# Joined at the seam of two layers and in the second: stores on another queue, value rows in three places, held loads

## The chip, the cores and the metric

The kernel runs on one core of one Trainium2 chip. The metric is device microseconds of one execution. Lower is better. Times of single executions are read from runs of the whole kernel, and where time goes is read from one profiled execution.

## What is computed

One step of a two-layer streaming encoder over 512 new prompt frames and 8 running streams of 16 frames each (640 rows of 2048). Layer 0 is stick-breaking attention with 16 heads and a cache; layer 1 is gated linear attention (GLA) with 4 heads, head widths 256 (keys) and 512 (values). The change touches the seam between the layers and layer 1:

```python
x = x + gate * y                                  # end of layer 0; per row
h = rmsnorm(x, norm_g) * (1 + scale) + shift      # start of layer 1
q, k, v, r, a_lr = split(h @ w_in)                # GLA products
g = log_sigmoid(a_lr @ w_a2 + b_a) / 16           # per-token decay
# Joined at the seam of two layers and in the second: stores on another queue, value rows in three places, held loads
a = tril((q * exp(b)) @ (k * exp(-b)).T)
o = a @ v + (q * exp(b)) @ S
S = exp(b_last) * S + (k * exp(b_last - b)).T @ v
```

Every float32 product is made of three matmuls on a high part and a low remainder (wh, wl, h and so on).

## The kernel before

One long function issues everything. TensorE's order (PE in the profile) is written out by a planner in the kernel: "lanes" are Python generators that yield a step with a wished delay, and a side scheduler puts their matmuls between those of the big products when the delay is over in its own count of time. The number in `step(2.8 ...)` is such a delay. ScalarE (ACT), VectorE (DVE) and GpSimd (POOL) keep the order that comes out of the recording in the parts around the change, and SyncE (SP) issues most DMAs in its order. Each engine works strictly in its own order, so an instruction that must wait holds up all that stands behind it on that engine. SP and ACT issue DMAs through hardware queues, POOL through a software queue (the helper `move`, L78). The DMAs of SP and ACT share a set of completion semaphores in rotation. A new DMA that gets a semaphore waits until the DMA that had it before has landed.

Three places matter.

**The seam (the part from L1235 on).** `add` (L1333) works on the 640 rows in five tiles (a = 0 to 4) and the 2048 columns in four groups (c = 0 to 3). VectorE makes x1 (L1336 to L1338), ScalarE sums its squares (L1340, tile junk) and then stores the tile to memory from its own queue (L1341, tile x<-y, 256 KB each, 20 in all). `turn` (L1316) lets TensorE transpose the tile (L1320) and ScalarE copy it out (L1322, xp). After the last group `norm` (L1325) reduces the squares (L1328), takes the root on VectorE and GpSimd (L232, L234, L243) and has TensorE turn the row factors (L248). ScalarE also casts the weights of layer 0's output product (L134, wh<-wr), and VectorE makes their remainder (L135, wl). `most` (L1295) prepares layer 1's input for rows 128 and up, `rest` that of the first 128 rows.

**The value jobs.** Layer 1's input product goes job by job, one of 256 output columns each (L595 matmuls, 170 a job). ScalarE's copy `m` (L608) stands once in each job. After a value job `keep_value` (L1451) has TensorE transpose the result in three pieces (g = 0, 1, 2; L681, ten transposes), ScalarE casts each into a tile kr and VectorE makes the remainder (L135, kr<-ps_tp,kr). SP stores both from kr (L74, gv<-kr, six stores a job). All three pieces use the same two slots, 12 and 13, so a piece can only be cast when the stores of the piece before have landed. Between these steps VectorE prepares the weights of the job after: t (L558), wb (L559, L562), and combines products: u and out (L601). The pool w5 (L1492) holds the tiles wa2r and wa2, which are used ahead of the value jobs only.

**The start of the GLA stage.** Here the last products (L654, copies pl at L1528, stores gq<-pl from ScalarE's queue at L1530) run beside the lanes `decays` (L1627 on: sums and exponentials of the gates of one head, es at L1673, for two halves dt = 0, 1), `prompt_lane` and `sample_lane` (L1819 on). SP loads v, q, k, three gate tiles (L1602) and weights (wr). POOL loads the first eight recurrent states (L1808, s<-in_state_gla, 256 KB each) and value rows of the samples (vst).

Of the kernel before, what the change touches and what calls it, by code (L numbers as in the profile page):

```python
# [26 lines left out]
GH = 4  # L27
# [14 lines left out]
def hybrid_step_kernel(ctx: ExitStack, tc: tile.TileContext, A: dict, O: list):  # L42
# [1200 lines left out]
    with tc.tile_pool(name="o0", bufs=1, reuse_waits="tile") as po, ExitStack() as only_d:  # L1243
# [81 lines left out]
        def norm(a):  # L1325
            yield step(3.0)
            ss = po.tile([P, 1], F32, tag="ss", name="ss", bufs=2)
            dve.tensor_reduce(out=ss, in_=ss4[:, a, :], axis=mybir.AxisListType.X, op=ALU.add)  # L1328
            wide = wide_of(po, rstd_of(po, ss, D, "nrm"))
            yield step(2.8 if a else 4.5, tp=1)  # L1330
            turned_wide(wide, bc, a)

        def add(a, c, pt):  # L1333
            xs, g = got[c]
            y = y_t[a, c]
            dve.tensor_tensor(y, pt, y, op=ALU.add)  # L1336
            dve.tensor_tensor(y, y, g[:, a // 4, :], op=ALU.mult)
            dve.tensor_tensor(y, y, xs[a], op=ALU.add)  # L1338
            junk = pd.tile([P, 512], BF16, tag="junk", name="junk", bufs=1)
            act(junk, y, AF.Square, accum_out=ss4[:, a, c:c + 1])  # L1340
            nc.scalar.dma_start(out=x1_d[a][:, 512 * c:512 * c + 512], in_=y)  # L1341
            if c == 3:
                side.add(counted(norm(a), a))
            side.add(counted(turn(a, c, y), a))
            busy["of"] += c > 0
# [105 lines left out]
        def keep_value(h, n):  # L1451
            def leave(out):
                def f(g, m, tp):
                    parts = [slot(12 + d, (P, 2, 256), name="kr")[:, :m, :] for d in range(2)]
                    halves(*parts, tp)
                    for d in range(2):
                        dst = gv_d[h][d][256 * g:256 * g + P * m, 256 * n:256 * n + 256]
                        store(dst.rearrange("(a p) n -> p a n", p=P), parts[d].bitcast(F32))
                side.add(as_rows(out, f))
            return leave  # L1460
# [28 lines left out]
        ring3["n"] = 1  # L1489
        ring3["pool"] = only_d.enter_context(tc.tile_pool(name="w2", bufs=1, reuse_waits="tile"))  # L1490

        wa_in = only_d.enter_context(tc.tile_pool(name="w5", bufs=1, reuse_waits="tile"))  # L1492
        r, wa2 = (wa_in.tile([96, GH * 256], t, name=n) for n, t in (("wa2r", F32), ("wa2", F32R)))
        for n in range(6):
            load(r[16 * n:16 * n + 16, :], A["gla_w_a2"][0])
        nc.scalar.copy(wa2, r)
# [20 lines left out]
    with tc.tile_pool(name="gl", bufs=1, reuse_waits="tile") as gl, \  # L1517
# [79 lines left out]
            act(on, o, AF.Copy, scale=r)  # L1597
            return on

        def gate(h, t0, tag, bufs):  # L1600
            g = gl.tile([P, 4, P], F32, tag=tag, name="gate", bufs=bufs)
            load(g, gr_d[h][:, :, t0:t0 + P])  # L1602
            return g

# [22 lines left out]
        def decays():  # L1627
# [8 lines left out]
            for h in range(GH):  # L1636
# [11 lines left out]
                for dt in range(2):  # L1648
                    n = 2 * h + dt
                    ba = cols[:, 48 + n:49 + n]  # L1650
                    b, y = (gl.tile([P, T], F32, tag=n, name=n) for n in ("b", "y"))
                    for c in hs:
                        yield step(0.0, tp=1)
                        pt = bank("tp")[:, :HALF]
                        l = wa2[:, P * dt:P * dt + P]
                        mm(pt, l, by(l, alr[:, c]), start=True, stop=True)
                        act(b[:, c], pt, AF.Abs, bias=ba)
                        dve.tensor_scalar(y[:, c], pt, ba, 0.0, op0=ALU.add, op1=ALU.min)
                    yield step(0.8)
                    act(b, b, AF.Exp, scale=-1.0)  # L1660
                    act(b, b, AF.Ln, bias=1.0)
                    yield step(1.7)
                    dve.tensor_tensor(y, y, b, op=ALU.subtract)
                    dve.tensor_tensor_scan(b, reset, y, 0.0, ALU.mult, ALU.add)
                    yield step(1.7)
                    bp = b[:, :NP].rearrange("p (c t) -> p c t", t=P)
                    bs = b[:, NP:].rearrange("p (c t) -> p c t", t=NT)
                    b1 = bp[:, :, 63:64].rearrange("p c o -> p (c o)")
                    bl = bp[:, :, 127:128].rearrange("p c o -> p (c o)")
                    act(e1[:, dt], b1, AF.Exp, scale=IT)  # L1670
                    act(el[:, dt], bl, AF.Exp, scale=IT)
                    dve.tensor_tensor(ed[:, dt], bl, b1, op=ALU.subtract)
                    act(es[:, dt], bs[:, :, 15:16].rearrange("p c o -> p (c o)"), AF.Exp, scale=IT)  # L1673
                    m = gl.tile([P, 4], F32, tag="m", name="m")
                    dve.tensor_copy(m, b1)
                    act(ed[:, dt], ed[:, dt], AF.Exp, scale=IT)
                    dve.tensor_tensor(bp, bp, m.unsqueeze(2).to_broadcast([P, 4, P]), op=ALU.subtract)
                    yield step(0.8)
                    for x, sign, f in ((q, 1.0, 1.0 / 16.0), (k, -1.0, 1.0)):
                        act(y, b, AF.Exp, scale=sign * IT)  # L1680
                        yield step(0.8)
                        dve.scalar_tensor_tensor(x[:, dt], x[:, dt], f, y, op0=ALU.mult, op1=ALU.mult)
                yield step(3.0 if h else 6.0)
                ready[h] = q, k, e1, el, ed, es
                if h + 1 < GH:
# [2 lines left out]
        def prompt_lane():  # L1688
# [6 lines left out]

            def fetch_gate(u):
                if u < len(units):
                    gs[u] = gate(units[u][0], P * units[u][1], "gp", GP)

            fetch(0)  # L1700
            side.after(10.0, lambda: fetch(1))
            for u in range(GP):
                side.after(14.0 + 2.0 * u, lambda u=u: fetch_gate(u))
            left = None

            def state(S, e1, dt, c):
# [30 lines left out]
                return a, kr  # L1737

            made, stored = None, 0.0
            for u, (h, c) in enumerate(units):  # L1740
                while h not in ready:
                    yield step(0.5)
# [60 lines left out]
        def ask():  # L1803
            x = next(asked, None)
            if x:
                h, e, dt, m = x
                s0 = gl.tile([P, 512], F32, tag="s0", name="s0", bufs=S0)
                move(s0, A["state_gla"][0, 2 * m + e, h, P * dt:P * dt + P, :])  # L1808
                states[x] = s0, pe["now"]

        for n in range(S0):
            side.after(18.0 + 2.0 * n, ask)

        def leaves(x):
            h, e, dt, m = x
# [3 lines left out]
        def sample_lane():  # L1819
            def fetch(h):  # L1820
                v = values(h, 4, "vn", 1)

                for e in range(2):
                    for i in range(3):
                        rows = gv_d[h][int(i == 1)][NP:, :].rearrange("(m e t) n -> e t m n", m=4, e=2)[e]
                        r0 = 64 * e + NT * i
                        move(vst[r0:r0 + NT].bitcast(F32), rows)
                return v, gate(h, NP, "gn", 1)

            yield step(12.0)  # L1830
            here = fetch(0)
            for h in range(GH):
                v, g = here
# [131 lines left out]
                yield step(0.5)  # L1965

        side.every = 1.0
        for x in (decays(), prompt_lane(), sample_lane(), fetches()):
            side.add(x)
        drive(others)  # L1970
        for g in range(2):
# [108 lines left out]
```

## Time and profile before

| what | value |
|---|---|
| median of 3 runs | 2503.4 us (2503.1 to 2503.6) |
| the profiled execution | 2511.72 us, of it the span 2510.0 us |
| granted TensorE clock, mean | 0.985 |
| busy: PE, DVE, ACT, POOL | 2426.9, 1580.7, 993.3, 139.8 us |
| moved by DMA | 502.07 MB, mean 200 GB/s |

The profile page gives busy times of the engines over the span, the granted TensorE clock, DMA load, the chain of work that ended last, and groups of instructions. Further views list the waits of an engine with what ended each, the instructions of an engine in order of time (start, duration, idle time before it in brackets with the releaser), and busy times of single stretches.

### The profile page before, as it was taken

Reading aid. Unit: us, or ns where it says so; the run is one execution under the profiler, and the core shown is the slowest. Engines: PE = TensorE matmul, PEld = TensorE weight load, DVE = VectorE, ACT = ScalarE, POOL = GpSimd, SP = SyncE. Lnnn points to the kernel's source line nnn. Section 1 sums busy time; section 2 is a strip of 40 time slices with the busy share of each in tenths; the row PEclk is TensorE's granted clock in tenths of the full one; section 3 lists DMA queues with packets and bytes.
Section 4 is the critical chain, followed back from the end, with each engine's and each line's share of the span. In section 5 each row is a group of like instructions: output and inputs, shape, how many; then the busy total and the mean of one; then the engine's idle time right before and its main releaser. Section 6 shows DMA issues by size and latency. Waiting matters only on the chain.

```text
span 2510.0 us, 43986 instructions
## 1 busy us (share of the span) xinstructions
PE 2426.9 (97%) x17561; PEld 2150.6 (86%) x17561; DVE 1580.7 (63%) x2566; ACT 993.3 (40%) x1731; POOL 139.8 (6%) x371
## 2 busy tenths in 40 slices
PE   6899999999999999999999989999999999999998
PEld 4589999999999999888887768999999989977776
DVE  5575555655556655676776578665676566665556
ACT  4342222222223335555443345333333455565223
POOL 0010000000000000000000000000000212332000
PEclk8899999999999999999999999999999999999999
DMA  9966666667654347877764655344443768976634
GB/s 343 330 204 223 217 209 212 221 214 223 214 194 128 112 152 255 268 235 244 254 214 154 195 201 154 108 117 130 130 116 108 210 201 263 293 265 207 221 114 147
DMA packets 470863, 502.07 MB, mean 200 GB/s; under 512 B 26107, under 2 KB 370563, under 8 KB 470531
## 3 DMA queue, kind: packets, MB, share of 16 engines
q1 hardware_dynamic: 440338, 440.80, 55.4%
q0 software_dynamic: 12848, 41.43, 4.7%
q10 hardware_dynamic: 17472, 17.04, 2.0%
q8 instruction: 138, 2.26, 0.4%
q14 instruction: 67, 0.54, 0.1%
HBM read 410.05 MB, written 89.13 MB: 199 GB/s over the span
## 4 chain that ended last, share of the span: by engine, by line
PE 77%; DMA 6%; DVE 5%; ACT 3%; issue 2%; SPq 0%; POOL 0%; ACTq 0%; POOLq 0%; DVEq 0%
PE ps_mm L595 39%; PE ps_mm L654 9%; PE ps_mm L700 9%; PE ps_mm L369 3%; PE ps_tp L1093 2%; DMA gv<-kr 2%; PE ps_tp L1568 2%; PE ps_mm L519 1%; PE ps_tp L1145 1%; PE ps_tp L1049 1%; PE ps_z L1025 1%; PE ps_z L180 1%; PE ps_mm L2051 1%; PE ps_z L1107 1%; PE ps_z L222 1%
## 5 line engine op out<-in xcount | busy, mean ns | idle before, releaser
L595 PE MATMUL ps_mm<-sums,wh 128*128 128x320 f32 x2752 | 613.7, 311 | 1.5 <-ACT wh L134 1.5
L595 PE MATMUL ps_mm<-h,wh 128*128 128x320 f32 x2064 | 463.1, 313 | 7.1 <-DVE u L601 7.1
L595 PEld LDWEIGHTS ps_mm<-sums,wh 128*128 128x128 f32 x2752 | 458.2, 188 | 10.4 <-issue 7.0
L595 PE MATMUL ps_mm<-sums,wl 128*128 128x320 f32 x1376 | 425.9, 310 | 0.7 <-DVE wl L135 0.7
L135 DVE TENSOR_TENSOR wl<-wr,wh 128x1024 fp32r<-128x1024 f32 x193 | 236.2, 1225 | 232.5 <-ACT wh L134 231.8
L595 PEld LDWEIGHTS ps_mm<-h,wh 128*128 128x128 f32 x2064 | 344.3, 189 | 23.5 <-issue 12.7
L134 ACT CAST wh<-wb 128x1024 fp32r<-128x1024 f32 x170 | 178.4, 1049 | 428.9 <-PE ps_mm L595 356.6
L134 ACT CAST wh<-wr 128x1024 fp32r<-128x1024 f32 x193 | 202.6, 1050 | 331.8 <-PE ps_mm L595 187.3
L595 PE MATMUL ps_mm<-h,wl 128*128 128x320 f32 x1032 | 320.0, 310 | 0.0
L654 PE MATMUL ps_mm<-h,wh 128*128 128x320 f32 x1152 | 266.1, 318 | 6.7 <-ACT pl L1528 4.0
L595 PEld LDWEIGHTS ps_mm<-sums,wl 128*128 128x128 f32 x1376 | 258.4, 188 | 1.0 <-DVE wl L135 1.0
L135 DVE TENSOR_TENSOR wl<-wb,wh 128x1024 fp32r<-128x1024 f32 x170 | 207.8, 1222 | 62.1 <-ACT wh L134 61.7
L654 PEld LDWEIGHTS ps_mm<-h,wh 128*128 128x128 f32 x1152 | 194.3, 190 | 21.3 <-issue 8.9
L700 PE MATMUL ps_mm<-wh,ogh 128*128 128x512 f32 x450 | 198.4, 441 | 8.2 <-ACT y L708 4.8
L595 PEld LDWEIGHTS ps_mm<-h,wl 128*128 128x128 f32 x1032 | 194.4, 188 | 0.0
L654 PE MATMUL ps_mm<-h,wl 128*128 128x320 f32 x576 | 179.3, 311 | 0.0
L700 PE MATMUL ps_mm<-wl,ogh 128*128 128x512 f32 x450 | 178.5, 397 | 0.8 <-DVE wl L135 0.8
L700 PE MATMUL ps_mm<-wh,ogl 128*128 128x512 f32 x450 | 178.6, 397 | 0.3 <-DVE ogl L135 0.3
L700 PEld LDWEIGHTS ps_mm<-wh,ogh 128*128 128x128 f32 x450 | 85.8, 191 | 37.1 <-issue 14.8
L654 PEld LDWEIGHTS ps_mm<-h,wl 128*128 128x128 f32 x576 | 109.3, 190 | 0.0
L700 PEld LDWEIGHTS ps_mm<-wh,ogl 128*128 128x128 f32 x450 | 85.3, 190 | 20.3 <-DVE ogl L135 0.7
L519 PE MATMUL ps_mm<-wh,h 128*128 128x512 f32 x252 | 93.1, 430 | 5.0 <-ACT h L134 3.0
(364 smaller groups left out, 3711.1 us busy)
## 6 DMA issues: line engine op xcount, KB each, us to landing
ar<-in_w_ada_dram SPq DMA_DIRECT2D x160, 512.0 KB
wb<-in_sb_w_in_dram SPq DMA_DIRECT2D x82, 512.0 KB
kc<-in_cache_sb_k_dram SPq DMA_DIRECT2D x64, 512.0 KB
vc<-in_cache_sb_v_dram SPq DMA_DIRECT2D x64, 512.0 KB
wr<-in_gla_w_in_dram SPq DMA_DIRECT2D x51, 512.0 KB
wb<-in_gla_w_in_dram SPq DMA_DIRECT2D x45, 512.0 KB
wr<-in_sb_w_in_dram SPq DMA_DIRECT2D x44, 512.0 KB
ar<-in_w_ada_dram SPq DMA_DIRECT2D x64, 256.0 KB
```

Source lines behind the costliest of these rows:

```text
L134: nc.scalar.copy(hi, x)
L135: (e or dve).tensor_tensor(lo, x, hi.bitcast(F32), op=ALU.subtract)
L180: mm(acc[32 * q:32 * q + 32, :w], cT[:, kt + m, :], by(cT[:, kt + m, :], rs[m // each][:, m % each, q, :]), start=kt + m == 0, stop=kt + m ...
L222: mm(acc[32 * j:32 * j + 32, :256], cT[:, kt + m, :], by(cT[:, kt + m, :], r[:, 256 * j:256 * j + 256]), start=kt + m == 0, stop=kt + m == ...
L369: mm(acc[a], l[:, c], by(l[:, c], r[:, k2, :]), start=kt == k0 and first, stop=kt == k0 + nk - 1 and last)
L519: mm(acc[a], l, by(l, r[:, e, :]), start=j == 0 and e == 0 and begun, stop=j == 7 and e == 1 and last)
L595: mm(acc, l[:, k, :], by(l[:, k, :], r), start=start and k == 0 and first, stop=k == 7 and last, skip_group_check=True)
L654: mm(acc[nt], l[:, k, :], by(l[:, k, :], r), start=k0 == 8 and k == 0 and first, stop=k0 == 0 and k == 7 and last)
L700: mm(acc, l, by(l, r[:, e, :]), start=i == 0 and e == 0 and first, stop=i == 1 and e == 1 and last)
L1025: mm(z[:, :n], q[:, hh, qs], by(q[:, hh, qs], k[:, hh, :n]), start=True, stop=True)
L1093: turn_block(tp[:, P * c:P * c + P], block(kc[:, c, P * hh:P * hh + P]), ident)
L1568: mm(out, l[a], by(l[a], r[b]), start=start and n == 0, stop=stop and n == 2, skip_group_check=True)
```

## The change

The joined pieces come to four edits, in the three places above.

- In `add`, the x1 stores of the first three column groups (15 DMAs) are issued by POOL in place of ACT; those of the last group stay on ACT.
- In `norm`, the delay ahead of the turning of the row factors is 1.6 in place of 2.8 for a = 1 to 4.
- In `keep_value`, the pieces g = 1 and g = 2 are cast into the tiles wa2r and wa2, each of which holds both parts of a piece. The piece g = 0 keeps the slots 12 and 13.
- At the start of GLA, the first two prompt gates, the first sample gate and the first eight states are not loaded by a timed delay: the lanes wait until `decays` has come to the second half of head 0, and a copy of one column of es into the tile (on POOL) makes the load wait for that value on the chip as well.

```diff
@@ -1327,7 +1327,7 @@
             ss = po.tile([P, 1], F32, tag="ss", name="ss", bufs=2)
             dve.tensor_reduce(out=ss, in_=ss4[:, a, :], axis=mybir.AxisListType.X, op=ALU.add)
             wide = wide_of(po, rstd_of(po, ss, D, "nrm"))
-            yield step(2.8 if a else 4.5, tp=1)
+            yield step(1.6 if a else 4.5, tp=1)
             turned_wide(wide, bc, a)
 
         def add(a, c, pt):
@@ -1338,7 +1338,7 @@
             dve.tensor_tensor(y, y, xs[a], op=ALU.add)
             junk = pd.tile([P, 512], BF16, tag="junk", name="junk", bufs=1)
             act(junk, y, AF.Square, accum_out=ss4[:, a, c:c + 1])
-            nc.scalar.dma_start(out=x1_d[a][:, 512 * c:512 * c + 512], in_=y)
+            (nc.gpsimd if c < 3 else nc.scalar).dma_start(out=x1_d[a][:, 512 * c:512 * c + 512], in_=y)
             if c == 3:
                 side.add(counted(norm(a), a))
             side.add(counted(turn(a, c, y), a))
@@ -1451,7 +1451,11 @@
         def keep_value(h, n):
             def leave(out):
                 def f(g, m, tp):
-                    parts = [slot(12 + d, (P, 2, 256), name="kr")[:, :m, :] for d in range(2)]
+                    if g:
+                        t = rows_in.tile([P, 1024], F32R, tag=("wa2r", "wa2")[g - 1], name="kr")
+                        parts = [t[:, 512 * d:512 * d + 256 * m].rearrange("p (a n) -> p a n", a=m) for d in range(2)]
+                    else:
+                        parts = [slot(12 + d, (P, 2, 256), name="kr")[:, :m, :] for d in range(2)]
                     halves(*parts, tp)
                     for d in range(2):
                         dst = gv_d[h][d][256 * g:256 * g + P * m, 256 * n:256 * n + 256]
@@ -1489,8 +1493,8 @@
         ring3["n"] = 1
         ring3["pool"] = only_d.enter_context(tc.tile_pool(name="w2", bufs=1, reuse_waits="tile"))
 
-        wa_in = only_d.enter_context(tc.tile_pool(name="w5", bufs=1, reuse_waits="tile"))
-        r, wa2 = (wa_in.tile([96, GH * 256], t, name=n) for n, t in (("wa2r", F32), ("wa2", F32R)))
+        rows_in = only_d.enter_context(tc.tile_pool(name="w5", bufs=1, reuse_waits="tile"))
+        r, wa2 = (rows_in.tile([P, GH * 256], t, tag=n, name=n)[:96] for n, t in (("wa2r", F32), ("wa2", F32R)))
         for n in range(6):
             load(r[16 * n:16 * n + 16, :], A["gla_w_a2"][0])
         nc.scalar.copy(wa2, r)
@@ -1597,8 +1601,10 @@
             act(on, o, AF.Copy, scale=r)
             return on
 
-        def gate(h, t0, tag, bufs):
+        def gate(h, t0, tag, bufs, behind=None):
             g = gl.tile([P, 4, P], F32, tag=tag, name="gate", bufs=bufs)
+            if behind is not None:
+                nc.gpsimd.tensor_copy(g[:, 0, 0:1], behind)
             load(g, gr_d[h][:, :, t0:t0 + P])
             return g
 
@@ -1680,6 +1686,8 @@
                         act(y, b, AF.Exp, scale=sign * IT)
                         yield step(0.8)
                         dve.scalar_tensor_tensor(x[:, dt], x[:, dt], f, y, op0=ALU.mult, op1=ALU.mult)
+                    if h == 0 and dt == 1:
+                        came["behind"] = es[:, 1, 0:1]
                 yield step(3.0 if h else 6.0)
                 ready[h] = q, k, e1, el, ed, es
                 if h + 1 < GH:
@@ -1695,12 +1703,10 @@
 
             def fetch_gate(u):
                 if u < len(units):
-                    gs[u] = gate(units[u][0], P * units[u][1], "gp", GP)
+                    gs[u] = gate(units[u][0], P * units[u][1], "gp", GP, came["behind"] if u < GP else None)
 
             fetch(0)
             side.after(10.0, lambda: fetch(1))
-            for u in range(GP):
-                side.after(14.0 + 2.0 * u, lambda u=u: fetch_gate(u))
             left = None
 
             def state(S, e1, dt, c):
@@ -1737,6 +1743,10 @@
                 return a, kr
 
             made, stored = None, 0.0
+            while "behind" not in came:
+                yield step(0.5)
+            for u in range(GP):
+                fetch_gate(u)
             for u, (h, c) in enumerate(units):
                 while h not in ready:
                     yield step(0.5)
@@ -1805,11 +1815,20 @@
             if x:
                 h, e, dt, m = x
                 s0 = gl.tile([P, 512], F32, tag="s0", name="s0", bufs=S0)
+                if len(states) < S0 and not begun_states:
+                    nc.gpsimd.tensor_copy(s0[:, 0:1], came["behind"])
                 move(s0, A["state_gla"][0, 2 * m + e, h, P * dt:P * dt + P, :])
                 states[x] = s0, pe["now"]
 
-        for n in range(S0):
-            side.after(18.0 + 2.0 * n, ask)
+        begun_states = []
+
+        def first_states():
+            while "behind" not in came:
+                yield step(0.5)
+            for n in range(S0):
+                ask()
+                yield step(0.5)
+            begun_states.append(True)
 
         def leaves(x):
             h, e, dt, m = x
@@ -1825,9 +1844,10 @@
                         rows = gv_d[h][int(i == 1)][NP:, :].rearrange("(m e t) n -> e t m n", m=4, e=2)[e]
                         r0 = 64 * e + NT * i
                         move(vst[r0:r0 + NT].bitcast(F32), rows)
-                return v, gate(h, NP, "gn", 1)
-
-            yield step(12.0)
+                return v, gate(h, NP, "gn", 1, None if h else came["behind"])
+
+            while "behind" not in came:
+                yield step(0.5)
             here = fetch(0)
             for h in range(GH):
                 v, g = here
@@ -1965,7 +1985,7 @@
                 yield step(0.5)
 
         side.every = 1.0
-        for x in (decays(), prompt_lane(), sample_lane(), fetches()):
+        for x in (decays(), first_states(), prompt_lane(), sample_lane(), fetches()):
             side.add(x)
         drive(others)
         for g in range(2):
```

**VectorE in a value job** (the first of six; kr are the pieces of the value rows, u and t belong to the product and to the next weights):

```order
 L135 TENSOR_TENSOR wl<-t_17317,wh 128x1024
-L135 TENSOR_TENSOR kr<-ps_tp,kr 128x512
+L135 TENSOR_TENSOR kr<-ps_tp,kr 128x512 x2
 L601 TENSOR_TENSOR u<-ps_mm,m_17377 128x320
 L135 TENSOR_TENSOR wl<-wb,wh 128x1024
-L135 TENSOR_TENSOR kr<-ps_tp,kr 128x512
-L135 TENSOR_TENSOR wl<-wr,wh 128x1024
 L135 TENSOR_TENSOR kr<-ps_tp,kr 128x256
-L558 TENSOR_TENSOR t_17571<-wb 128x1024
+L135 TENSOR_TENSOR wl<-wr,wh 128x1024
+L558 TENSOR_TENSOR t_17569<-wb 128x1024
 L601 TENSOR_TENSOR u<-ps_mm,m_17377 128x320
```

The second piece now stands ahead of u, and the third one ahead of the remainder wl of wr instead of directly ahead of t. The other five jobs change in the same way.

**ScalarE at the seam**, before and then after, around the cast of the weights wr that the prediction speaks of (junk is the sum of squares, x_0 a store of x1, xp the copies out of the transposes):

```order
L1341 DMA x_4_90<-y 128x512
L1322 COPY xp<-ps_tp 128x2x128 x2
L1340 ACTIVATE junk,ss_15146<-y 128x512
L1341 DMA x_0_86<-y 128x512
L134 CAST wh<-wr 128x1024
L1322 COPY xp<-ps_tp 128x2x128 x4
```

```order
L1340 ACTIVATE junk,ss_15146<-y 128x512 x2
L1322 COPY xp<-ps_tp 128x2x128 x2
L1340 ACTIVATE junk,ss_15146<-y 128x512
L134 CAST wh<-wr 128x1024
L1322 COPY xp<-ps_tp 128x2x128 x4
```

The casts and copies stand as they stood; the stores between them are gone. On POOL they stand ahead of the five nrm_r of the row norms.

**SP at the start of GLA**, before and then after (gate are the three gate tiles, wr the weights of the last products):

```order
L71 DMA v<-gv_1_108 128x512
L71 DMA gate<-gr_103 128x4x128 x3
L71 DMA wr<-in_gla_w_in_dram 128x8x128 x2
L71 DMA wa_20976<-wa_d 96x256
L71 DMA wr<-in_gla_w_in_dram 128x8x128 x2
L71 DMA q<-gq_96 128x1280
```

```order
L71 DMA wr<-in_gla_w_in_dram 128x8x128
L71 DMA v<-gv_1_108 128x512
L71 DMA wr<-in_gla_w_in_dram 128x8x128
L71 DMA wa_20972<-wa_d 96x256
L71 DMA wr<-in_gla_w_in_dram 128x8x128
L71 DMA gate<-gr_103 128x4x128 x3
L71 DMA wr<-in_gla_w_in_dram 128x8x128
L71 DMA q<-gq_96 128x1280
```

Three weight loads now stand ahead of the gates, and one weight load and the load of q behind them. On POOL the eight state loads stand behind the loads of vst, with eleven copies from es (three into gates, eight into state tiles) around the first of them.

## The prediction

> **What bounds the kernel now.** I read the page first, then TensorE's waits, then each of the three places in order of time. The page's busy line:
>
> ```profile
> PE 2426.9 (97%) x17561; PEld 2150.6 (86%) x17561; DVE 1580.7 (63%) x2566; ACT 993.3 (40%) x1731; POOL 139.8 (6%) x371
> ```
>
> PE is the bound. The change gives PE neither fewer matmuls nor shorter ones, so it can only win where PE stands idle or runs at a reduced clock. PE's waits (total, times, longest) name the places:
>
> ```profile
> PE ps_mm L595 <- DVE u L601: 7.1, 6, 2.0
> ...
> PE ps_tp L1320 <- ACT xp L1322: 4.3, 3, 2.1
> PE ps_mm L654 <- ACT pl L1528: 4.0, 2, 3.8
> ```
>
> The first is the value jobs, the second the seam, the third the start of the GLA stage. Together they are 15.4 us, 0.6% of 2503.4. A fifth of a per cent, 5 us, is about what a measurement can tell from no change.
>
> **A: the x1 stores leave ACT's queue.** Following the chain back from 1445 us leads to a load of adaLN weights (ar), and from it to ACT and PE:
>
> ```profile
> 1437.85 5.70 DMA ar<-in_w_ada_dram
> ```
> ```profile
> 1443.94 1.04 ACT L134 CAST wh<-wr 128x1024 fp32r<-128x1024 f32 x1 [2.86 <-DMA ar<-in_w_ada_dram]
> ```
> ```profile
> 1445.58 1.12 PE L1320 MATMUL ps_tp<-ident,y 128*128 128x128 f32 x4 [2.10 <-ACT xp L1322]
> ```
> ```profile
> 1445.58:1449.06 3.48, 3.48 (x10) 2.57 (x10) 3.38 (x6) 1.17 (x5) 0.00 (x0) 0.53 0.60 155
> ```
>
> The cast wh reads wr, not ar. What stands ahead of it on ACT is the store at L1341: it has to wait for its turn on a completion semaphore that the load of ar still holds until 1443.55. So ACT stands 2.86 us, its copies xp come late, and PE stands 2.10 us. Then PE runs 3.48 us at clock 0.53 (last row, the stretch's seventh figure), which loses (1 - 0.53) x 3.48 = 1.64 us. With the store on POOL, the cast starts 2.86 us earlier, the copies too, and PE's 2.10 us are covered with some 0.7 to spare. Gain: 2.10 + 1.64 = **3.7 us**. If another wait stands there, it is 0. The 15 issues leave ACT, which is idle over half the time, so they are worth nothing by themselves. On POOL they stand ahead of the row norms' small steps, but POOL has nothing else there, and the stores of group 3, whose end the norms follow, stay on ACT.
>
> [...]
>
> **The shorter delay in `norm`.** VectorE at the end of the seam, then PE:
>
> ```profile
> 1482.02 0.16 DVE L1328 TENSOR_REDUCE ss<-ss 128x1 f32<-128x4 f32 x1 [0.51 <-ACT junk L1340]
> ...
> 1487.56 1.14 DVE L256 SCALAR_TENSOR_TENSOR xp<-xp,sc,rstd_bc 128x384 f32<-128x384 f32 x2
> ```
> ```profile
> 1485.32 0.50 PE L519 MATMUL ps_mm<-wh,h 128*128 128x512 f32 x1 [2.09 <-ACT h L134]
> ```
>
> The planner turns a = 1 to 3 three matmuls earlier and puts the norm of a = 0 (L1328, L232, POOL's root, L243) behind the first set of `most` instead of ahead of it. The first set can start up to 1.4 us sooner, and with it PE's L519. But the same four steps, about 1.3 us with POOL's answer, then delay the second set (the second row), and everything behind it. I take **0**, bounds -0.5 (the four steps and a copy xp that stands ahead of a cast) and +1.4.
>
> **B: the value rows in three places.** Three stretches: a gate job without any wait of PE, the six value jobs together (from one copy m to the seventh), and the worst of them. Columns: length, PE busy, ..., clock, DMA share, GB/s.
>
> ```profile
> 1616.74:1641.38 24.64, 24.64 (x171) 24.63 (x171) 15.66 (x16) 8.00 (x11) 0.00 (x0) 1.00 0.34 86
> 1641.38:1804.17 162.79, 157.37 (x1069) 155.88 (x1069) 103.24 (x116) 56.69 (x75) 0.00 (x0) 0.99 0.47 130
> 1694.08:1723.58 29.50, 27.50 (x180) 27.25 (x180) 17.10 (x19) 9.23 (x13) 0.00 (x0) 0.94 0.42 116
> ```
>
> A matmul takes 24.64 / 171 = 0.144. A value job has ten transposes more, whose price a job without disturbance shows:
>
> ```profile
> 1752.52 0.60 PE L681 MATMUL ps_tp<-ident,out 128*128 128x128 f32 x4
> 1752.88 0.54 PE L595 MATMUL ps_mm<-sums,wh 128*128 128x320 f32 x2
> 1753.26 0.31 PE L595 MATMUL ps_mm<-sums,wl 128*128 128x320 f32 x1
> ```
>
> Four cost 1753.26 - 1752.52 - 2 x 0.144 = 0.45, ten 1.13. An undisturbed value job is 24.64 + 1.13 = 25.77, six are 154.6. They take 162.79, so 8.2 us are lost: 162.79 - 157.37 = 5.4 as idle PE, the rest in slow clock. The mechanism in the worst job, on DVE, then PE:
>
> ```profile
> 1708.25 0.42 DVE L135 TENSOR_TENSOR kr<-ps_tp,kr 128x256 fp32r<-128x256 f32 x1 [3.64 <-DMA gv<-kr]
> 1708.59 1.22 DVE L558 TENSOR_TENSOR t<-wb 128x1024 f32<-128x1024 f32 x1
> 1709.72 0.48 DVE L601 TENSOR_TENSOR u<-ps_mm,m 128x320 f32<-128x320 f32 x1
> ```
> ```profile
> 1710.35 0.53 PE L595 MATMUL ps_mm<-h,wh 128*128 128x320 f32 x2 [2.00 <-DVE u L601]
> ```
>
> The third piece kr waits 3.64 us for the stores of the second, since both use the same tiles. Behind it on DVE stand t and u, and u empties the bank that PE needs. With a place for each piece, a piece waits only for the same piece's stores of the job before, 26 us old, so kr no longer waits. What is next late? t needs the weights wb. DVE's waits over all these jobs:
>
> ```profile
> DVE u L601 <- PE ps_mm L595: 15.0, 10, 1.6
> DVE kr L135 <- DMA gv<-kr: 13.7, 9, 3.6
> ...
> DVE t L558 <- DMA wb<-in_gla_w_in_dram: 2.4, 3, 0.9
> ```
> ```profile
> 1700.93 0.37 SPq L71 DMA_DIRECT2D wb<-in_gla_w_in_dram  x1
> ```
>
> wb left at 1700.93, 6.85 us into the job. In the new order on SP it stands behind two stores that it stood ahead of, one of them the store of the third piece's cast; without the waits for old stores that cast comes early enough that the load leaves no later than now. t cost PE 2.00 by starting at 1708.59, 14.5 into the job, so it costs nothing up to 12.5: the load has 5.7 us. The second piece's remainder, now ahead of u, takes at most twice the 0.42 of the half as wide third one, in a time in which DVE waits up to 1.6 for PE (first row). I take the whole **8.2 us**, lower bound 5.4 (idle alone).
>
> [...]
>
> **C: the held loads.** The chain of the last wait goes back to a load of v, in a stretch (1970 to 1990) with the DMA engines full:
>
> ```profile
> 1978.66 14.52 DMA v<-gv
> ```
> ```profile
> 1970.00:1990.00 20.00, 19.32 (x132) 19.09 (x131) 9.37 (x14) 7.37 (x14) 7.30 (x16) 1.00 0.98 321
> ```
>
> ACT and PE behind it:
>
> ```profile
> 1988.54 0.53 ACT L1657 ACTIVATE b<-ps_tp,cols 128x320 f32<-128x320 f32 x1
> ...
> 1993.62 1.28 ACT L1660 ACT_TABLE_LOAD   x1 [4.54 <-DMA v<-gv]
> ...
> 2005.29 0.41 ACT L1528 COPY pl<-ps_mm 128x320 f32<-128x320 f32 x1
> ...
> 2010.45 0.20 ACT L1673 ACTIVATE es<-b 128x8 f32<-128x8 f32 x1
> ```
> ```profile
> 2005.75 0.90 PE L654 MATMUL ps_mm<-h,wh 128*128 128x320 f32 x2 [3.80 <-ACT pl L1528]
> ```
> ```profile
> 2005.70:2008.90 3.20, 3.15 (x12) 3.15 (x13) 1.81 (x6) 3.16 (x5) 0.00 (x0) 0.54 0.57 153
> ```
>
> Ahead of the table load stands the store gq, which waits for the semaphore of a v load that took 14.52 us behind two megabytes of states and three gates. ACT could have gone on at 1988.54 + 0.53 = 1989.07 and did at 1993.26, 4.2 us later. With states and gates held, the v loads have the DMA engines almost to themselves; ACT's chain moves 4.2 us ahead, and pl is copied at 2001.1, against PE's need at 2001.95: the 3.80 us go, and with them (1 - 0.54) x 3.15 = 1.45 of slow clock. Of 5.25 I take **5.0**, since the spare is only some 0.4; the bounds are 0 and 5.25.
>
> What the hold costs: es comes at 2010.45 - 4.2 = 2006.3. Until then SP stands at the first gate, and behind it a weight load and q; POOL stands at its first copy, and behind it the eight state loads. Three weight loads stand ahead of the gates, and PE's next after those comes later. From 2007 on 11 x 256 KB and 0.5 MB of weights, 3.3 MB, take some 10 us at 321 GB/s. PE first uses a state in
>
> ```profile
> L1885 PE MATMUL ps_z<-s,qz x32: 592/605/617, 2037.4 to 2075.8; 128*32 128x512 f32 x32
> ```
>
> at 2037.4, or about 2032 after the shift, so 15 us of slack cover it. If the cover were gone, each microsecond of lateness would cost one.
>
> **Sum.** 3.7 + 0 + 8.2 + 5.0 = 16.9 us, from 2511.7 to 2494.8 in the profiled execution. That one lies 8.3 above the median; the terms are waits between engines, which I take over unchanged: 2503.4 - 16.9 = **2486.5**.
>
> **Rivals.**
> 1. [...] Chance 0.07.
> 2. *C does not do what it says*: the store gq draws another load that lands late, or the SP queue behind the gates delays weights by what ACT won. C is 0, the time 2491.5. For it: the spare of 0.4 us. Chance 0.12.
> 3. *B gives half*: the second piece ahead of u makes u late when ACT casts it late. 4.1 less, 2490.6. Chance 0.08.
> 4. *The seam gives more*: the first set comes sooner and POOL's answer delays nothing, so that PE's wait of 2.09 at 1485 goes and with it a slow stretch like that of A (1.64): 3.7 less than forecast, 2482.8. For it: the wait of DVE for the norm of a = 0 stood right ahead of the set. Against: the four steps are only moved. Chance 0.10.
> 5. *The wait passes on to the weights, slower than before*: in all six value jobs t waits for wb, which now stands behind stores. If each job loses what the worst loses today, 29.50 - 25.77 = 3.73, that is 22.4 in place of 8.2, +14.2 against the 8.7 of A and C: 2508.9. It decides once the load takes over 5.7 us, and reaches this price at 7.7. For it: the 5.70 of a load of the same size above. Against: DVE waited for wb 0.9 at most. Chance 0.03.
> 6. Two of 1 to 3 at once, about 2495: 0.04. Nearly everything eaten by new waits, within 5 us of before: 0.04.
>
> **How the numbers follow.** The forecast keeps 0.52. The range reaches from rival 4 with C's upper bound and the 0.5 us by which the runs of before differ, 2482.0, past two failing at once, to 2496; that leaves out the last of 6 and rival 5. Faster by over 0.2%: 0.52 + 0.07 + 0.12 + 0.08 + 0.10 + 0.04 = 0.93; same 0.04; slower 0.03.
>
> **What the profile after would show.** Right: no wait of ACT for ar ahead of wh at the seam; kr without DMA waits and six value jobs in about 155 us; no table load waiting for v and PE's wait for pl gone; states landing before 2032. Wrong: wb as the releaser of t in several jobs, PE waiting for wr behind the gates, or POOL's nrm_r behind stores.

## The result, and the profile after

The changed kernel takes 2486.14 us (median of 5 runs, 2483.16 to 2488.68), the kernel before 2503.40 (5 runs, 2500.94 to 2504.13). That is 17.3 us less, ratio 0.9928 with a 95% interval of 0.9916 to 0.9940. Measured once more later, the ratio is 0.9930 (0.9918 to 0.9942). The forecast was 2486.5. Its sum came out, but not all of its terms, and what follows is mostly about that.

The profiled execution of after took 2488.44 us, its span 2486.7, at a mean clock of 0.990. TensorE's waits in it (total, times, longest):

```profile
PE ps_mm L519 <- ACT h L134: 6.6, 4, 3.0
...
PE ps_tp L1883 <- DVE kc L1878: 2.4, 1, 2.4
...
PE ps_z L1283 <- DMA ar<-in_w_ada_dram: 1.8, 3, 0.9
...
PE ps_mm L654 <- ACT pl L1532: 1.0, 1, 1.0
PE ps_tp L1320 <- ACT xp L1322: 0.7, 1, 0.7
```

The waits for u (7.1) are gone, those for xp fell from 4.3 to 0.7 and those for pl from 4.0 to 1.0. New are a wait of 2.4 for kc and 1.5 more for ar, and the wait for h at L519 grew from 4.4 to 6.6.

**The value jobs.** The stretch of the six jobs, with the columns as in the prediction, then DVE in the third job and SP's load of wb:

```profile
1633.15:1787.56 154.41, 154.41 (x1069) 154.31 (x1069) 103.54 (x116) 57.33 (x75) 0.00 (x0) 1.00 0.48 137
```
```profile
1687.02 0.69 DVE L135 TENSOR_TENSOR kr<-ps_tp,kr 128x512 fp32r<-128x512 f32 x1 [0.44 <-ACT kr L134]
...
1690.24 0.42 DVE L135 TENSOR_TENSOR kr<-ps_tp,kr 128x256 fp32r<-128x256 f32 x1
...
1696.07 1.23 DVE L558 TENSOR_TENSOR t<-wb 128x1024 f32<-128x1024 f32 x1 [1.97 <-DMA gv<-kr]
```
```profile
1690.35 0.37 SPq L71 DMA_DIRECT2D wb<-in_gla_w_in_dram  x1
```

PE is busy through all of the 154.41 us (162.79 before; 154.6 was forecast). No kr waits for a store. What waits now is t, about 2 us in every job. The view names a store of kr as what ended it in four of the six jobs and the load of wb in two. The landing times in the trace settle it for the load: in each of the six jobs wb lands 0.08 us before t starts, and the last store of kr lands 0.2 to 0.3 us after that start. In the job shown t starts 11.45 us into the job (the copy m stands at 1684.62), in the first of the six 12.2, and by the prediction's working PE does not notice before 12.5. The load leaves 5.7 us into the job shown, and t starts 5.7 after that. So the fifth rival's mechanism is there in part, and a slack of about 1 us (0.3 in the first job) keeps it from PE.

**The seam.** ACT around the cast that had stood 2.86 us, and then where PE stands instead: the chain of waits, PE, and the stretch of that load, with its clock, DMA share and GB/s in the last three columns.

```profile
1435.83 0.63 ACT L1340 ACTIVATE junk<-y 128x512 bf16<-128x512 f32 x1 [0.80 <-DVE y L1338]
1436.36 0.19 ACT L1340 ACTIVATION_READ_ACCUMULATOR junk<-y 128x1 f32 x1
1436.46 1.03 ACT L134 CAST wh<-wr 128x1024 fp32r<-128x1024 f32 x1
```
```profile
1449.48 10.31 DMA ar<-in_w_ada_dram
```
```profile
1459.83 0.64 PE L1283 MATMUL ps_z<-ar,c 128*32 128x256 f32 x8 [0.60 <-DMA ar<-in_w_ada_dram]
```
```profile
1449.50:1459.80 10.30, 8.57 (x56) 5.55 (x56) 6.29 (x11) 4.19 (x13) 1.43 (x3) 1.00 1.02 379
```

The cast follows the sums at once and PE has no gap at this place. The 15 stores show on the queues: q10 (hardware_dynamic) carried 17.04 MB in before and 13.11 now, q0 (software_dynamic) 41.43 and 45.36. But PE, now 3.8 us further on than before, catches up with the loads of ar. A load of ar refills a tile that PE has just used, so PE's lead makes the two loads that it later waits for leave 3.8 us earlier, counted from the first matmul of the stage. They land only 1.3 to 1.4 us earlier, in a stretch with the DMA engines full (a share of 1.02 at 379 GB/s), and one takes 10.31 us. In before the same two had landed 1.1 and 0.2 us ahead of their use.

**The start of the GLA stage.** ACT, PE, and the load that ACT waits for later:

```profile
1971.92 0.53 ACT L1663 ACTIVATE b<-ps_tp,cols 128x320 f32<-128x320 f32 x1
...
1972.47 1.28 ACT L1666 ACT_TABLE_LOAD   x1
...
1984.15 0.41 ACT L1532 COPY pl<-ps_mm 128x320 f32<-128x320 f32 x1
...
2006.14 1.04 ACT L134 CAST wh<-wr 128x1024 fp32r<-128x1024 f32 x1 [4.37 <-DMA wr<-in_gla_w_in_dram]
```
```profile
1989.88 0.56 PE L654 MATMUL ps_mm<-h,wh 128*128 128x320 f32 x2 [1.04 <-ACT pl L1532]
...
2008.69 0.44 PE L1883 MATMUL ps_tp<-ident,kc 128*128 128x128 f32 x2 [2.41 <-DVE kc L1878]
```
```profile
1993.20 12.86 DMA wr<-in_gla_w_in_dram
```

The table load waits for nothing, pl comes in time, and the 3.80 us are gone. But the weight wr that stands behind the gates on SP leaves at 1993.20 together with the gates and states, and takes 12.86 us. ACT's cast waits 4.37 for it, kc stands behind the cast, and PE waits 2.41 and runs slow after it (two rows under "The slow clock" below).

### The profile page after: what moved, and what is told of

Read it like the earlier page. It is cut to its first block, busy times and chain, and to the rows that moved or that the text cites. A ratio compares the mean times of both kernels' runs of the same rounds, so it can differ in the third digit from the quotient of the medians.

```text
span 2486.7 us, 44040 instructions
## 1 busy us (share of the span) xinstructions
PE 2418.2 (97%) x17561; PEld 2146.8 (86%) x17561; DVE 1580.0 (64%) x2566; ACT 994.3 (40%) x1731; POOL 151.9 (6%) x397
## 3 DMA queue, kind: packets, MB, share of 16 engines
q0 software_dynamic: 14048, 45.36, 5.3%
q10 hardware_dynamic: 15312, 13.11, 1.6%
## 4 chain that ended last, share of the span: by engine, by line
PE 82%; DVE 3%; DMA 3%; ACT 2%; issue 2%; POOL 0%; SPq 0%; ACTq 0%; POOLq 0%; DVEq 0%
PE ps_mm L595 42%; PE ps_mm L700 10%; PE ps_mm L654 8%; PE ps_mm L369 3%; PE ps_tp L1572 2%; PE ps_tp L1093 2%; PE ps_tp L1049 1%; PE ps_tp L1145 1%; PE ps_z L1025 1%; PE ps_z L180 1%; PE ps_mm L2071 1%; PE ps_z L222 1%; PE ps_z L1107 1%; PE ps_tp L681 1%; PE ps_mm L519 1%
## 5 line engine op out<-in xcount | busy, mean ns | idle before, releaser
L519 PE MATMUL ps_mm<-wh,h 128*128 128x512 f32 x252 | 90.9, 422 | 5.6 <-ACT h L134 4.7
```

What stands on the lines that cost most here:

```text
L519: mm(acc[a], l, by(l, r[:, e, :]), start=j == 0 and e == 0 and begun, stop=j == 7 and e == 1 and last)
```

## The experiments

Single executions differ by several microseconds in places that no edit touches: up to 1420 us into the kernel, where all are the same, the profiles lie up to 4.7 us apart, and the first profile of before is the slowest of them. So I measured stages. Each stage is bounded by the same matmuls in every execution (at 1420, 1516, 1641, 1804, 1976, 2040, 2200 and 2340 us in the first profile of before), and the table gives by how much it is shorter than in that profile, from the matmuls' start times.

| execution | seam 1420-1516 | values 1641-1804 | GLA start 1976-2040 | late 2200-2340 |
|---|---|---|---|---|
| before, again | 3.0 | 2.6 | -2.8 | -0.5 |
| stores alone | 2.3 | 0.3 | -2.4 | 4.3 |
| delay alone | 2.4 | 0.9 | -1.2 | 4.2 |
| seam (both) | 3.1 | 0.5 | -0.8 | 6.1 |
| values alone | 1.0 | 8.3 | -1.6 | 3.3 |
| held alone | 0.7 | 3.6 | 2.8 | 5.1 |
| after | 3.3 | 8.4 | 0.3 | 6.5 |
| after, again | 2.3 | 8.4 | 3.4 | 7.0 |
| after, long delay | 3.7 | 8.4 | 3.4 | 5.1 |
| after, gates held only | 1.6 | 8.4 | 0.3 | 0.6 |
| after, states held only | 3.0 | 8.4 | 4.5 | 5.7 |
| the same, again | 3.7 | 8.4 | 4.5 | 5.4 |
| after, states later | 3.6 | 8.4 | 4.5 | 4.7 |

Ratios below are to before on the same chip, with 95% intervals, and microseconds won are worked out from the ratio.

### The pieces one by one

**The seam's two edits alone.**

```diff
-            yield step(2.8 if a else 4.5, tp=1)
+            yield step(1.6 if a else 4.5, tp=1)
...
-            nc.scalar.dma_start(out=x1_d[a][:, 512 * c:512 * c + 512], in_=y)
+            (nc.gpsimd if c < 3 else nc.scalar).dma_start(out=x1_d[a][:, 512 * c:512 * c + 512], in_=y)
```

> Before with the seam's two edits alone (x1 stores of three column groups on POOL, the shorter delay in norm). Theory 1, the terms of the prediction: 3.7 us less than before, all at 1445, ACT's wait of 2.86 ahead of the cast wh gone. Theory 2, the sum of what the two profiles show: about 3.6 less as well. [...] The late stretch (PE from 2220 to 2330, in the time of before) as in before, if its 6.6 us come from the held loads; less long, if it is a knock-on of being earlier.

Median 2499.97 against 2505.36, ratio 0.9985 (0.9974 to 0.9995): 3.8 us less, between 1.3 and 6.5.

**The value rows alone** (the edits in `keep_value` and in pool w5).

> Before with the value rows in three places alone. Both theories: six value jobs in about 154.5 us in place of 162.8, 8.3 us less in the median, no DVE wait of kr for gv. If it gains more than 9, the late stretch (2220 to 2330) has gained with it and is a knock-on of being earlier.

2498.51 against 2505.36, 0.9976 (0.9966 to 0.9986): 6.0 us less, 3.5 to 8.5. The stage is 8.3 shorter than in the first profile of before, as expected, but that profile was the slowest there. Over six executions with the old `keep_value` the stage is 1.3 shorter on average (0, 2.6, 0.3, 0.9, 0.5, 3.6), so the edit brings some 7.

**The held loads alone** (the edits in `gate`, `decays` and the lanes).

> Before with the held loads alone. Theory 1: 5.0 us less, PE's 3.80 us wait for pl gone and nothing in its place. Theory 2: PE is some 5 us earlier at 2005, and has lost that again by 2035, because the weight load behind the held gates lands late and ACT's cast waits over 4 us for it; in the whole 0 to 0.5 us, unless the late stretch is shorter because of the hold, then about 5 us.

2496.05 against 2505.36, 0.9966 (0.9953 to 0.9980): 8.5 us less, 5.0 to 11.8, more than either theory said. PE's and ACT's waits from 1940 to 2130 us, one view each:

```profile
PE ps_tp L1879 <- DVE kc L1874: 1.5, 1, 1.5
PE ps_mm L654 <- ACT pl L1528: 1.0, 1, 1.0
```
```profile
ACT wh L134 <- DMA wr<-in_gla_w_in_dram: 3.5, 1, 3.5
```

The weight is late here too, and PE loses 1.7 of the 4.5 us that it had won by 2015. And the late stretch is 5.1 shorter.

**The kernel before once more.**

> The kernel before once more, for its profile. If the late stretch is the same in each execution, PE waits again 2.3 us for s (L1893) and 4.8 us for y (L708) between 2220 and 2330. If these are a matter of the single execution, they differ, and the 6.6 us between the two profiles there belong to no edit.

It took 2507.49. PE's waits at the start of the GLA stage and in the late stretch:

```profile
PE ps_mm L654 <- ACT pl L1528: 6.6, 1, 6.6
```
```profile
PE ps_mm L700 <- ACT y L708: 4.2, 2, 2.3
PE ps_tp L1891 <- DVE s L1893: 4.1, 1, 4.1
```

The late stretch is as in the first profile, but the wait for pl is 6.6 in place of 3.8. In the six executions without any hold, ACT waited 4.5, 7.3, 6.6, 4.5, 5.3 and 6.2 for v. The profile that the prediction read had one of the two shortest.

### Which half of the seam

**The stores alone.**

```diff
-            nc.scalar.dma_start(out=x1_d[a][:, 512 * c:512 * c + 512], in_=y)
+            (nc.gpsimd if c < 3 else nc.scalar).dma_start(out=x1_d[a][:, 512 * c:512 * c + 512], in_=y)
```

> Before with only the x1 stores of three column groups on POOL; the delay in norm is as before. Theory 1 (the prediction's terms): the stores alone bring the 3.7 us, the delay nothing, so this is as fast as both together (2500.0 against 2505.4 there), ratio 0.998 to 0.999. Rival: the shorter delay brings part of it, then this one gains under 2 us, and PE's wait for xp at the end of the seam (1.5) is still there.

2504.20 against 2503.79, ratio 0.9998 (0.9988 to 1.0008): nothing that can be measured, up to 3 us less. PE's waits at the seam:

```profile
PE ps_mm L519 <- ACT h L134: 2.8, 2, 2.1
PE ps_z L1283 <- DMA ar<-in_w_ada_dram: 2.6, 3, 1.6
PE ps_tp L1320 <- ACT xp L1322: 2.2, 2, 1.5
```

The wait of 2.1 for xp at 1445 is gone (4.1 to 4.8 in all for xp without either edit, 2.2 here), and the wait for ar is 2.6 in place of 0.3 to 0.7. The wait for xp at the end of the seam (1.5) is still there, as the rival had it. The wait at 1445 was passed on to the loads.

**The shorter delay alone** (the first of the two hunks above, on before).

> Before with only the shorter delay in norm. The prediction's term: 0, at most 1.4 us. Rival from the first two seam runs (both edits 5.4 us under before, the stores alone 0): the delay brings 2 to 4. In the profile PE's wait for xp at the end of the seam (1.5) is gone and its wait for h there is 1 to 2 longer.

2503.45 against 2505.78, ratio 0.9987 (0.9978 to 0.9997): 3.3 us less, 0.8 to 5.5. PE's waits at the seam:

```profile
PE ps_mm L519 <- ACT h L134: 4.6, 2, 2.7
PE ps_tp L1320 <- ACT xp L1322: 3.0, 2, 2.3
```

The wait for xp at the end of the seam (1.5) is gone and that for h is about 1 us longer (3.0 to 3.7 in the four unedited executions), as expected.

**After with the long delay.**

```diff
-            yield step(1.6 if a else 4.5, tp=1)
+            yield step(2.8 if a else 4.5, tp=1)
```

> After with the delay of before (2.8). By the prediction's term the same as after within 1.4 us. If the delay brings 2 to 4 us (rival), this is that much slower than the run of after beside it.

2489.57, beside 2488.42 for after; ratios to before 0.9937 (0.9924 to 0.9950) and 0.9930. The intervals overlap, so here the delay is worth 1.2 us or nothing. In the stage table the seam is 2.3 and 3.7 shorter with the stores, 2.4 with the delay, and 1.6 to 3.7 with both (mean 2.9 of seven); unedited it is 0 to 3.0 shorter (mean 1.2 of four). Each edit seems to free some of the same 1 to 2 us, and they do not add. How much belongs to which stays open within these intervals.

### Which half of the hold, and the late weight

**Only the gates held**, the states by the timed delay as in before:

```diff
-                if len(states) < S0 and not begun_states:
-                    nc.gpsimd.tensor_copy(s0[:, 0:1], came["behind"])
...
+        for n in range(S0):
+            side.after(18.0 + 2.0 * n, ask)
```

> After, but the first eight states are loaded by the timed delay as before; only the three gates are held. Theory 1, the states (2 MB) crowd the v loads: ACT waits for v ahead of the table load by 3 to 6 us as before, PE for pl by 3 to 5, and the kernel is 2 to 4 us slower than after. Rival, the gates crowd them: ACT does not wait, PE's wait for pl stays at 1.0. In both the weight wr behind the gates lands in time, since the states are not in flight with it, so PE's wait for kc (2.4 after) is gone.

2493.53, ratio 0.9960 (0.9946 to 0.9973), some 7 us above after, where 2 to 4 were expected. PE's waits at the start of GLA, then ACT's for v:

```profile
PE ps_mm L654 <- ACT pl L1532: 2.7, 2, 1.5
PE ps_tp L1662 <- DMA wa<-wa_d: 2.1, 1, 2.1
```
```profile
ACT L1666 <- DMA v<-gv: 1.9, 1, 1.9
```

ACT's wait for v is shorter than in before (4.5 to 7.3) but not gone, and a load of wa is late as well. So ACT waits 1.9 for v with the states alone in flight, and 4.5 to 7.3 with both. The weight behind the gates is on time, as both theories had it. In the table this version is 0 to 3 behind after at the start of GLA and 6 behind in the late stretch.

**Only the states held**, the gates by the timed delay as in before:

```diff
-                return v, gate(h, NP, "gn", 1, None if h else came["behind"])
+                return v, gate(h, NP, "gn", 1)
...
+            for u in range(GP):
+                side.after(14.0 + 2.0 * u, lambda u=u: fetch_gate(u))
```

> After, but the three gates are loaded by the timed delay as before; only the states are held. Theory 1: v has the queues nearly to itself (0.77 MB of gates in place of 2.8 MB), ACT waits for v at most 1.5 us and PE for pl about 1. The weight behind is not queued behind gates, but the states are in flight with it: it lands some 2.5 us earlier than after, PE's wait for kc falls from 2.4 to about 0. Median 1 to 4 us below after. Rival, the hold of the gates is what frees v: ACT waits over 3 us.

2486.01, ratio 0.9926 (0.9914 to 0.9938). ACT waits neither for v nor for wr, and PE from 1980 to 2016 only here:

```profile
1990.73 0.56 PE L654 MATMUL ps_mm<-h,wh 128*128 128x320 f32 x2 [1.04 <-ACT pl L1532]
```

So the gates alone in flight make ACT wait for nothing. The 4.5 us are kept to 2040.

**The states held longer**, by the scores of the second prompt unit, the gates held as in after:

```diff
-                    nc.gpsimd.tensor_copy(s0[:, 0:1], came["behind"])
+                    nc.gpsimd.tensor_copy(s0[:, 0:1], came["later"])
...
                     made = scores(u + 1)
+                    came.setdefault("later", made[0][0][:, 0:1].bitcast(F32))
```

> After, but the eight states wait for a later value, the scores of the second prompt unit (aTh, about 10 us after es), so that the weight load issued behind the gates has only 0.77 MB of gates beside it. Theory 2: ACT's wait for wr (4.4 us after) and PE's for kc (2.4) go, the 4.2 us that were given back between 2015 and 2040 are kept, and the median is about 4 below after, near 2482 (ratio 0.991); the states still land before their first use. Rival, wr is late because SP stood at the gates: ACT's wait falls by under 2 us. Rival, the states come late: PE waits at L1906 for s.

2488.70, ratio 0.9937 (0.9923 to 0.9950). In the stage the theory holds: the weight is in time although it stands behind the gates, the waits for wr and kc are gone and 4.5 us are kept. So it was the states in flight that made wr late, not the standing of SP. The whole is not faster than after, though some 4 us were expected.

**After once more, and beside it only the states held.**

> The changed kernel once more, beside the next one on the same chip. If the 4.2 us that its first profile gives back between 2015 and 2040 belong to the kernel, ACT waits again 3 to 5 us for the weight wr there and PE 1.5 to 2.4 for kc; if they were a matter of that one execution, they are absent. Ratio to before 0.992 to 0.994. PE from 2222 to 2330 again some 5 us shorter than in before.

> After with only the states held, once more, for a direct comparison. If wr's lateness costs 2 to 4 us in each execution of after, this is 2 to 4 us faster than the run beside it; if it is 1 us or less, the late weight is made up later in after, or comes only in some executions.

2488.42 (0.9930) and 2487.28 (0.9921, interval 0.9908 to 0.9934). In this execution of after ACT waited 2.8 for wr, PE 0.9 for kc, and 1.1 us were given back, not 4.2. Over the four profiles with both held, it is 4.2, 1.7, 1.2 and 1.1. So the late weight costs 1 to 4 us in an execution, and holding the states alone is 1.1 better in the median here, within the uncertainty. No version that was run is clearly faster than after.

### The late stretch

From 2200 to 2340 the profile of after is 6.5 shorter than the first one of before, where no edit stands. Before loses there by POOL's queue. The chain of waits, then ACT and PE:

```profile
2309.37 5.42 DMA out_dram<-s
...
2316.59 0.58 POOL on_r L234
```
```profile
2317.19 0.69 ACT L1597 ACTIVATE on<-ps_tp,on_r 128x512 f32<-128x512 f32 x1 [3.95 <-POOL on_r L234]
```
```profile
2318.99 0.60 PE L700 MATMUL ps_mm<-wh,ogh 128*128 128x512 f32 x1 [2.91 <-ACT y L708]
```

A state may only be loaded into its tile when the state stored from it has landed. POOL stands at that load, the root on_r stands behind it, ACT's copy y behind on_r, and PE waits 2.91. In after, ACT's wait at this place is:

```profile
2295.09 0.69 ACT L1601 ACTIVATE on<-ps_tp,on_r 128x512 f32<-128x512 f32 x1 [0.55 <-POOL on_r L234]
```

Over the fourteen profiles the stretch is shorter by -0.5 to 6.1 (mean 2.6) in the seven without held states and by 4.7 to 7.0 (mean 5.6) in the seven with them. Held states thus seem to be worth some 3 us here, perhaps by a shift in when POOL's stores and loads meet. Part of the 6.5 us between the first two profiles is slow clock: two slow stretches of 3.41 us, worth 1.7 each, stand there in before (from 2240.74 and 2319.25), one in after (from 2245.29). But the two groups overlap in one execution: the seam's edits alone, without any hold, had the stretch 6.1 shorter. Nothing was run that sets the shift by itself. It stays open.

## Why the prediction was right, and where its steps were not

**A, 3.7 forecast.** The mechanism was right: without the store ahead of it the cast comes at once, and PE's 2.10 us go. In the trace of before, the 1197 DMAs of SP and ACT name eight semaphores, 149 or 150 each, and the store left at 1443.57, 0.02 us after the load of ar that had the same one had landed. The step that failed is taking the 2.10 us as gained. What would be late next was not asked of the loads: PE comes earlier to ar, and waits 1.2 to 2.6 for it where it had waited 0.3 to 0.7. The 1.64 us of slow clock were not the kernel's either: the same wait for xp stands in four more profiles with the stores on ACT (1.77 to 2.41 us), and in the two of them whose transposes behind it were read, the delay alone and the value rows alone, these take 0.66 us in place of 1.12 (see the slow clock below). The stores alone measure 0.5 us less, and at most 3: the 2.86 us of standing did go, and little of the time with it.

**The delay, 0 forecast, bounds -0.5 and +1.4.** Alone it measured 3.3 less (0.8 to 5.5), in after 1.2 or nothing. PE's wait for xp (1.5) goes and the wait for h grows by 1, much as the working had it. Why it should be more than the bound of 1.4 is not shown: in its profile the seam is 2.4 shorter, within the 0 to 3.0 of the unedited executions. For both edits of the seam, 3.8 was measured, which is the sum forecast with its parts wrong.

**B, 8.2 forecast.** The mechanism is shown: kr waits for no store, and the six jobs take 154.4 to 154.5 in the eight executions with the edit, to 0.2 of the undisturbed length worked out. The size was that of one profile, the first of before, and the slowest there. Over six executions it is 7, in the medians 6.0 (3.5 to 8.5). The working put 2.8 of the 8.2 down to slow clock; the clock record has one slow stretch there (3.41 us from 1711.68), worth 1.7. The next late thing was named rightly: t is held up by wb in all six jobs, with about 1 us left, and 0.3 in the first.

**C, 5.0 forecast.** The first half is shown: in before the store gq left at 1993.26, 0.08 us after that load of v had landed; the holds free v, and PE is 4.5 us earlier by 2015 in each of the seven executions with the states held; against the mean of six without, which wait longer for v than the one I read, even 6.0. The step that failed is the cover: that PE's next weight after the three ahead of the gates "comes later". In the profile of after ACT was free for that weight at 2001.8, it landed at 2006.06, and PE stood from 2006.3; 1 to 4 us went back in the four profiles with both held. That is what the second half of rival 2 said, for which I had 0.12, though by the states in flight and not by the standing of SP. What was not forecast at all is the late stretch, which comes with the held states. Held loads alone measure 8.5.

**The sum.** 3.8, 6.0 and 8.5 of the pieces alone add up to 18.3, and together they bring 17.3 (18.0 by the ratio). Set against the means of the executions without the edit, the two profiles of after win 1.6 us at the seam, 7.1 in the values, 3.3 at the start of GLA and 4.2 in the late stretch. So in the stages that the forecast spoke of, some 12 of its 16.9 us came, and the late stretch, for which it had no term, made up most of the rest. That the sum met the median within 0.4 us is luck. The measured medians of the delay (3.3) and of the held loads (8.5) lie beyond their upper bounds of 1.4 and 5.25, and those of the stores and of B lie below their terms.

**The slow clock.** After the gap of 2.41 at 2008, too, PE ran slow. The same pair of matmuls ahead of it and behind it, in the profile of after:

```profile
2005.43 0.62 PE L1572 MATMUL ps_tp<-v,krh 128*128 128x512 f32 x2
...
2009.90 1.05 PE L1572 MATMUL ps_tp<-v,krh 128*128 128x512 f32 x2
```

Gaps of 2.1 and 2.4 us sufficed for it in these two places.

A gap of this length does not always bring it. With the value rows alone, PE waits at the place of A's 2.10 us even longer, and the stretch after it runs at full clock (seventh figure, 1.00 against 0.53); the same four transposes take 0.66 us against 1.12:

```profile
1443.96 0.66 PE L1320 MATMUL ps_tp<-ident,y 128*128 128x128 f32 x4 [2.41 <-ACT xp L1322]
```
```profile
1444.00:1447.48 3.48, 3.48 (x28) 2.31 (x29) 3.38 (x6) 1.17 (x5) 0.00 (x0) 1.00 0.61 162
```

The clock records of before and after show more. Between 100 and 2460 us before has nine slow stretches and after five; the first of each lasts 6.83 us, every other one 3.41, and within a trace they begin at whole multiples of 3.41 us from each other. I divided the two traces along this grid and took PE's busy share in every piece at full clock. Of 13 pieces with a share under 0.48, all 13 were followed by a slow piece; of 1348 with a share over 0.60, none was; of the 8 between, one was. In before, 1.96 of the 2.10 us lay in one piece, which ended at 1445.44 and had a share of 0.43; in after, 2.33 of the 2.41 lay in one that ended at 2009.77, with 0.32. Where the 2.41 us with the value rows alone lay on such a grid was not shown. But a gap of this length cost the 1.7 us more of a slow stretch in one execution and not in another.

## What to carry to other kernels

A wait of an engine on a DMA that it does not read is worth looking for: in both places here it was a store queued ahead that waited for its turn (2.86 and 4.54 us), and moving it, or holding the crowding transfers, freed the whole chain behind. But a gain read off one wait is an upper bound until the next transfer that the bound engine meets has been checked, with the time at which it will then be needed. And a term read off one execution may be several microseconds off; a second profile of the same kernel tells how much of a wait, and of the slow clock behind it, is the kernel's.

## What was not expected of the hardware

Landing times under load vary by more than a factor of two: a weight load took 5.70 us at the seam, 10.31 there when PE ran ahead, and 12.86 beside 2.8 MB of held loads. Stages in which PE waits for nothing repeat almost exactly: the six value jobs took 154.4 to 154.5 us in eight executions, while with the stores in the way they took between 159.2 and 162.8.
